# Low weight parts of layer 1 formed once in layer 0 and loaded, and the depthwise convolution on VectorE split by even and odd positions

## The chip, the cores and the metric

The kernel runs on one core of one Trainium2 chip. The metric is the device time of one execution in microseconds (us). "Before" is the kernel without the change, "after" the kernel with it. A difference is given in per cent of the time before.

## The reference

The reference takes an activation of 2048 positions by 1024 channels through two layers, in float32. Each adds to its input a mixer's output that was normalised (RMSNorm before the mixer and after it). Layer 0 is attention over a window of 128 positions and a pooling mixer. The change touches the second layer, whose mixer is:

```
def odd_mixer(h, w_in, dw_w, dw_b, ln_g, ln_b, w_out):
    proj = h @ w_in
    a, b, gate = jnp.split(proj, [CONV_WIDTH, 2 * CONV_WIDTH], axis=-1)
    glu = a * jax.nn.sigmoid(b)
    conv = lax.conv_general_dilated(
        glu, dw_w.astype(glu.dtype), window_strides=(1,), padding=[(CONV_K - 1, 0)],
        dimension_numbers=('NWC', 'WIO', 'NWC'), feature_group_count=CONV_WIDTH)
    cf = conv.astype(jnp.float32) + dw_b.astype(jnp.float32)
    mu = jnp.mean(cf, axis=-1, keepdims=True)
    var = jnp.mean(jnp.square(cf - mu), axis=-1, keepdims=True)
    cn = (cf - mu) * lax.rsqrt(var + EPS) * ln_g.astype(jnp.float32) + ln_b.astype(jnp.float32)
    y = jax.nn.silu(cn).astype(h.dtype) * jax.nn.silu(gate)
    return y @ w_out
```

`w_in` is 1024 x 3072, `w_out` 1024 x 1024, and the convolution has 31 taps for each of the 1024 channels. The norm over channels needs the convolution of all channels before one position can be finished.

## The kernel before

**Halves and blocks.** Positions are worked in two halves of 1024 (`NH`), each of two blocks of 512 (`NB`). Channels lie on the 128 partitions, in eight tiles (`KT`). Layer 0 runs through both halves (`inproj0`, `outproj(0, half)`), then layer 1: `inproj1(0)`, `gates1(0)`, `inproj1(1)`, `gates1(1)`, and after these `outproj(1, 0)` and `outproj(1, 1)`. TensorE's order of matmuls is this order.

**A projection in three matmuls.** Every float32 operand of a projection is split in a high part in a reduced format and a low part, the rest. `w_load` fetches one weight tile (`wr`, 128 x 8 x 128, 512 KB) after the other, in the order of a list `wseq`, through three buffers. `w_split` copies it on ScalarE to `wh` (line 373) and subtracts on VectorE to get `wl` (line 374), two buffers each. `project` (line 385) then does for each of the eight channel tiles three matmuls: `wh` by the high part of the activation, `wh` by its low part, `wl` by its high part. A tile of layer 1's input projection or gates (`wc`) serves both blocks of a half, 48 matmuls of 512 columns; a tile of the output projection (`wo1`) serves one block, 24 matmuls. So the 24 `wc` tiles are loaded and split twice, and the eight `wo1` tiles four times: 80 tiles in layer 1. The last block of the kernel (`last_block`) goes by two parts of 256 columns and keeps its eight tiles.

**The convolution.** For each channel tile `inproj1` projects `b` and `a`, and `glu` multiplies them into a tile `gl`. Five of the eight channel tiles are convolved on VectorE (`conv_dve`, line 1027): one multiply-add over 1024 positions for each tap, into two sums in turn, and an add that writes the result in another order of positions. It is stored in DRAM (`cd`). The other three go through TensorE with Toeplitz matrices (`conv_pe`), result `ct`. `gates1` makes SiLU of the gate and stores it (`sg`).

**The norm.** `norms(half)` loads the eight results again (`s<-cd`, `s<-ct`), adds them up (column sums on TensorE, tile `a`), subtracts the mean, sums squares, and spreads the root by TensorE (`pt` are column sums, `pv` what is spread). `apply` scales, takes SiLU, multiplies by the gate (`s<-sg`), and splits the mixed tile into `hi` and `lo`. These mixed tiles are what `outproj(1, half)` multiplies; `ready` there holds each matmul group until its tile is there. `norms(1)` starts only when eight of the sixteen mixed tiles (eight channel tiles, two blocks) of half 0 are done, as `dones[0]` says (line 1159).

**Who sets the order.** The instructions' order on each engine is fixed when the program is built. The code is written as tasks that yield; a planner (class `Flow`, line 54) runs the tasks against estimated costs and due times, and emits each engine's list of instructions by priority and readiness. So a change in one task's work moves other tasks' instructions. All loads and stores go through SP's queue, in the order of its list, and an instruction there that waits for a buffer holds all behind it. As every instruction is recorded by one wrapper, all carry line L189 in the profile (L190 in the changed kernel), and tiles are told apart by names: `mm` is the PSUM bank of a projection, `s` any tile of the common pool `s4` (37 slots of 1056 floats), `t` a small tile of 512.

## Time and profile before

| what | value |
|---|---|
| time, median of 3 runs | 1501.53 us (1500.33 to 1501.77) |
| profiled execution, its own time | 1503.71 us |
| its span in the trace | 1500.8 us |
| mean granted clock of TensorE | 0.991 |
| TensorE busy | 1469.3 us (98%) |
| VectorE busy | 1250.2 us (83%) |
| ScalarE busy | 565.2 us (38%) |
| DMA, share of 16 engines | 39.3% |

The span runs from the first to the last instruction that the profiler recorded; 2.9 us of the profiled execution lie outside it. A share of busy time is a mean over stages: layer 0 ends at about 675 us, layer 1's projections and gates at about 1260, the output projection of half 0 at about 1377, and the last block starts at about 1440. The granted clock is TensorE's, in parts of its full 2.4 GHz; 0.50 is its lower level of 1.2 GHz.

### The profile page before, as it was taken

Reading aid. Unit: us, or ns where it says so; the run is one execution under the profiler, and the core shown is the slowest. Engines: PE = TensorE matmul, PEld = TensorE weight load, DVE = VectorE, ACT = ScalarE, POOL = GpSimd, SP = SyncE. Lnnn points to the kernel's source line nnn. Section 1 sums busy time; section 2 is a strip of 40 time slices with the busy share of each in tenths; the row PEclk is TensorE's granted clock in tenths of the full one; section 3 lists DMA queues with packets and bytes.
Section 4 is the critical chain, followed back from the end, with each engine's and each line's share of the span. In section 5 each row is a group of like instructions: output and inputs, shape, how many; then the busy total and the mean of one; then the engine's idle time right before and its main releaser. Section 6 shows DMA issues by size and latency. Waiting matters only on the chain.

```text
span 1500.8 us, 19112 instructions
## 1 busy us (share of the span) xinstructions
PE 1469.3 (98%) x7226; PEld 1193.0 (79%) x7226; DVE 1250.2 (83%) x1927; ACT 565.2 (38%) x1069; POOL 49.1 (3%) x65
## 2 busy tenths in 40 slices
PE   8999999999999999999999999999999999998997
PEld 6877778788877778788888888888888888776796
DVE  7888775777887766577899999999999999989885
ACT  6454432454444423454211123211212134666551
POOL 0000000000000000000100000000000000000000
PEclk9999999999999999999999999999999999999898
DMA  6112312455411101355421224422544744836574
GB/s 221 57 54 80 97 44 59 140 175 176 145 33 33 46 29 56 99 178 187 166 63 55 82 85 136 172 71 67 182 148 137 236 144 137 256 127 229 165 251 154
DMA packets 107468, 186.46 MB, mean 124 GB/s; under 512 B 32240, under 2 KB 56432, under 8 KB 107376
## 3 DMA queue, kind: packets, MB, share of 16 engines
q1 hardware_dynamic: 107376, 185.25, 39.3%
q8 instruction: 56, 0.92, 0.3%
q14 instruction: 36, 0.29, 0.1%
HBM read 146.42 MB, written 38.80 MB: 123 GB/s over the span
## 4 chain that ended last, share of the span: by engine, by line
PE 92%; DVE 3%; DMA 2%; ACT 1%; issue 1%; SPq 0%; POOL 0%; POOLq 0%; DVEq 0%; ACTq 0%
PE mm L189 81%; PE a L189 5%; PE pv L189 3%; PE pt L189 2%; DVE s L189 2%; DMA s<-in_toep 1%; DVE t L189 1%; DVE wl L189 0%; DMA s<-in_xn 0%; DMA gt<-s 0%; ACT s L189 0%; DMA s<-sg 0%; SPq L189 0%; ACT wh L189 0%; ACT t L189 0%
## 5 line engine op out<-in xcount | busy, mean ns | idle before, releaser
L189 PE MATMUL mm<-s,wh 128*128 128x512 f32 (+1 forms) x3616 | 1139.6, 396 | 13.3 <-ACT s L189 7.4
L189 PEld LDWEIGHTS mm<-s,wh 128*128 128x128 f32 x3616 | 669.5, 189 | 164.6 <-DVE s L189 10.7
L189 PE MATMUL mm<-s,wl 128*128 128x512 f32 (+1 forms) x1808 | 709.9, 393 | 0.0
L189 PEld LDWEIGHTS mm<-s,wl 128*128 128x128 f32 x1808 | 341.4, 189 | 76.2
L189 DVE SCALAR_TENSOR_TENSOR s<-s,packed,s 128x1024 f32<-128x1024 f32 x290 | 354.6, 1279 | 0.0
L189 ACT ACTIVATE wh<-wr 128x1024 fp32r<-128x1024 f32 (+1 forms) x138 | 145.4, 1054 | 368.8 <-PE mm L189 315.9
L189 DVE TENSOR_TENSOR wl<-wr,wh 128x1024 fp32r<-128x1024 f32 (+1 forms) x138 | 167.7, 1215 | 74.9 <-ACT wh L189 72.8
L189 ACT ACTIVATE t<-mm 128x512 f32<-128x512 f32 (+1 forms) x122 | 68.5, 562 | 98.6 <-PE mm L189 90.3
L189 DVE TENSOR_TENSOR t<-t,t 128x512 f32<-128x512 f32 (+1 forms) x131 | 86.2, 663 | 17.3 <-ACT t L189 15.4
L189 ACT ACTIVATE s<-mm 128x512 f32<-128x512 f32 (+1 forms) x116 | 67.9, 585 | 78.2 <-PE mm L189 70.8
L189 PE MATMUL a<-s,s 128*128 128x128 f32 (+2 forms) x592 | 90.5, 290 | 1.1 <-DMA s<-in_toep 0.9
L189 PEld LDWEIGHTS a<-s,s 128*128 128x128 f32 x592 | 81.1, 190 | 11.1 <-DMA s<-in_toep 2.8
L189 DVE TENSOR_TENSOR s<-s,s 128x512 f32<-128x512 f32 (+3 forms) x100 | 85.0, 874 | 3.3 <-DMA s<-ct 1.0
L189 ACT ACTIVATE s<-t 128x512 fp32r<-128x512 f32 (+1 forms) x52 | 48.8, 938 | 64.4 <-DVE t L189 64.1
L189 DVE TENSOR_TENSOR s<-t,s 128x512 fp32r<-128x512 f32 (+1 forms) x56 | 52.4, 935 | 22.1 <-ACT s L189 20.9
L189 ACT ACTIVATE t<-s 128x512 f32<-128x512 f32 x80 | 48.8, 628 | 50.7 <-DVE s L189 42.4
L189 DVE TENSOR_TENSOR t<-pt,packed 128x512 f32<-128x512 f32 x64 | 44.1, 690 | 28.4 <-PE pt L189 27.9
L189 ACT ACTIVATE s<-s,st 128x128 f32<-128x128 f32 x128 | 49.6, 389 | 25.0 <-DVE st L189 24.9
L189 POOL TENSOR_TENSOR rs<-ms,mhalf 128x4 f32<-128x4 f32 (+1 forms) x21 | 24.9, 1186 | 791.8 <-DVE ms L189 787.7
L189 DVE SCALAR_TENSOR_TENSOR s<-t,mm 128x512 f32<-128x512 f32 x48 | 40.1, 836 | 8.1 <-PE mm L189 6.2
L189 ACT ACTIVATE s<-xh 128x512 fp32r<-128x512 f32 x48 | 29.9, 630 | 39.9 <-DVE xh L189 39.5
L189 PEld LDWEIGHTS pv<-t,s 128*64 128x64 f32 x480 | 25.1, 136 | 23.2 <-issue 7.2
(100 smaller groups left out, 928.3 us busy)
## 6 DMA issues: line engine op xcount, KB each, us to landing
wr<-in_wo SPq DMA_DIRECT2D x64, 512.0 KB, 3.7
wr<-in_wc SPq DMA_DIRECT2D x48, 512.0 KB, 3.7
wr<-in_wa SPq DMA_DIRECT2D x27, 512.0 KB, 3.7
s<-in_toep SPq DMA_DIRECT2D x24, 384.0 KB, 4.3
xr<-in_xp SPq DMA_DIRECT2D x32, 256.0 KB, 4.1
x<-s SPq DMA_DIRECT2D x32, 256.0 KB, 3.2
xh<-x SPq DMA_DIRECT2D x32, 256.0 KB, 3.6
sg<-s SPq DMA_DIRECT2D x16, 512.0 KB, 4.8
```

What stands on the lines that cost most here:

```text
L189: fn(*args, **kw)
```

## The change

**Low parts.** A new task `w_lows`, of low priority and due from 60 us on, forms the low part of each of the 32 different weight tiles of layer 1 during layer 0: a load of 512 KB, a copy on ScalarE, a subtraction on VectorE, a store of 512 KB into DRAM (`wcl_*`, `wo1l_*`). In layer 1 `w_split` no longer subtracts: it loads the low part into the `wl` buffer by SP's queue, 80 times, and copies `wh` as before.

**Convolution by parity.** `gl` holds its even and its odd positions apart. With x0, x1 the two and w0, w1 the even and odd taps, `conv_dve` forms x0 + x1 and three filters of 512 positions with 16, 15 and 16 taps: ya = w0 * x0, yb = w1 * x1, yc = (w0 + w1) * (x0 + x1). One parity of the result is ya + yb (shifted), the other yc - ya - yb. That makes one add of 527 elements, 47 multiply or multiply-add instructions of 512 or 513, and three adds of 512, of which two write in the changed order, where 31 instructions of 1024 and one add of 1024 stood. `glu` of these channel tiles becomes two instructions of half size.

**The norm's start and priorities.** `norms(1)` starts at `gated`, when all projections and gates are emitted, and no longer asks for eight mixed tiles of half 0; its loads run at most two ahead of the sums, its blocks have a priority one lower, and taking a slot waits until four are free or `gated`.

The diff, without the sizes of packed constants and the layout of the carried positions:

```diff
--- before.py
+++ after.py
...
@@ -320,6 +321,24 @@
     for h in range(NH):
         wseq += [("wo1", f) for b in range(NB) for f in range(KT)]
     wraw, wready, last = [], [], set()
+    lows = [x for n, x in enumerate(wseq) if x[0] in ("wc", "wo1") and x not in wseq[:n]]
+    kept = {(name, i): dr.tile([P, KT, P], F32, tag=f"{name}l_{i}", name=f"{name}l_{i}") for name, i in lows}
+    formed = set()
+
+    def w_lows():
+        yield 60.0
+        for name, i in lows:
+            yield from until(lambda: avail["s4"] > 5)
+            raw = (yield from get("s4")).rearrange("p (k f) -> p k f", k=KT)
+            wl = (yield from get("s4", TH, F32R)).rearrange("p (k f) -> p k f", k=KT)
+            yield Q.dma_start(out=raw, in_=a[name][i])
+            yield A.activation(wl, raw, AF.Copy)
+            at = V.tensor_tensor(out=wl, in0=raw, in1=wl.bitcast(F32), op=ALU.subtract)
+            put(raw)
+            yield at
+            Q.dma_start(out=kept[name, i], in_=wl.bitcast(F32))
+            put(wl)
+            formed.add((name, i))
 
     def w_load(go):
         for n, (name, i) in enumerate(wseq):
@@ -370,8 +389,12 @@
             for j, ks in enumerate(WPARTS if n == len(wseq) else WHOLE):
                 yield from until(lambda: len(at) > j)
                 yield at[j]
+                if (name, i) in kept:
+                    yield from until(lambda: (name, i) in formed)
+                    Q.dma_start(out=wl.bitcast(F32), in_=kept[name, i])
                 yield A.activation(wh[:, ks], raw[:, ks], AF.Copy)
-                V.tensor_tensor(out=wl[:, ks], in0=raw[:, ks], in1=wh[:, ks].bitcast(F32), op=ALU.subtract)
+                if (name, i) not in kept:
+                    V.tensor_tensor(out=wl[:, ks], in0=raw[:, ks], in1=wh[:, ks].bitcast(F32), op=ALU.subtract)
                 if j == 0:
                     wready.append((name, i, wh, wl))
             put(raw)
@@ -580,6 +603,7 @@
     rb0 = {}
     flow.spawn(w_load(go), 0)
     flow.spawn(w_split(), 0)
+    flow.spawn(w_lows(), 6)
     for b in range(NB):
         flow.spawn(prep_first(b, hs, have, go), 1 + b)
     flow.wait(lambda: len(go) == NB)
...
@@ -612,6 +638,10 @@
         G.memset(low, -1.0e37)
         V.tensor_scalar(nsink, sinks, -1.0, None, op0=ALU.mult)
         V.tensor_scalar(dwb, dwb, 2.0, None, op0=ALU.mult)
+        V.tensor_scalar(dwb2, dwb, 2.0, None, op0=ALU.mult)
+        pairs_of = dwn[:, :, 1:].rearrange("p i (m r) -> p i m r", r=2)
+        V.tensor_tensor(out=dws[:, :, 1:], in0=pairs_of[:, :, :, 0], in1=pairs_of[:, :, :, 1], op=ALU.add)
+        V.tensor_copy(dws[:, :, :1], dwn[:, :, :1])
         V.tensor_scalar(dwbp, dwbp, 2.0, None, op0=ALU.mult)
         yield at
         V.tensor_copy(upper, up[:, :P])
@@ -1024,22 +1054,38 @@
         for w in ws:
             put(*w)
 
+    def parities(gl):
+        return gl.rearrange("f (r j) -> f r j", r=2)
+
     def conv_dve(half, i, slot, gl, over):
-        acc = []
-        for _ in range(2):
-            acc.append((yield from get("s4")))
-        V.tensor_scalar(acc[0], gl[:, 0:TH], dwn[:, slot, 0:1], dwb[:, i:i + 1], op0=ALU.mult, op1=ALU.add)
-        yield flow.t["P"]
-        V.tensor_scalar(acc[1], gl[:, 1:1 + TH], dwn[:, slot, 1:2], None, op0=ALU.mult)
-        for k in range(2, CK):
-            yield flow.t["P"]
-            r = acc[k % 2]
-            V.scalar_tensor_tensor(r, gl[:, k:k + TH], dwn[:, slot, k:k + 1], r, op0=ALU.mult, op1=ALU.add)
+        n = TH // 2
+        even, odd = parities(gl)[:, 0, :], parities(gl)[:, 1, :]
+        ta = yield from get("s4", 2 * n + HJ)
+        tb = yield from get("s4", 2 * n + 1)
+        both, ya = ta[:, :n + HJ], ta[:, n + HJ:]
+        yb, yc = tb[:, :n + 1], tb[:, n + 1:]
+        V.tensor_tensor(out=both, in0=even, in1=odd, op=ALU.add)
+        for m in range(HJ + 1):
+            for r, x, w, bias in ((ya, even, dwn[:, slot, HIST - 2 * m:CK - 2 * m], dwb), (yb, odd, dwn[:, slot, HIST - 1 - 2 * m:HIST - 2 * m] if m < HJ else None, None), (yc, both, dws[:, slot, HJ - m:HJ + 1 - m], dwb2)):
+                if w is None:
+                    continue
+                yield flow.t["P"]
+                xs = x[:, HJ - 1 - m:HJ + n - m] if x is odd else x[:, HJ - m:HJ + n - m]
+                if m:
+                    V.scalar_tensor_tensor(r, xs, w, r, op0=ALU.mult, op1=ALU.add)
+                elif bias is None:
+                    V.tensor_scalar(r, xs, w, None, op0=ALU.mult)
+                else:
+                    V.tensor_scalar(r, xs, w, bias[:, i:i + 1], op0=ALU.mult, op1=ALU.add)
         put(gl)
         cf = yield from get("s4")
+        cv = cf.rearrange("f (q r s) -> f r s q", r=2, s=SG)
         yield flow.t["P"]
-        at = V.tensor_tensor(out=permuted(cf), in0=natural(acc[0]), in1=natural(acc[1]), op=ALU.add)
-        put(*acc)
+        V.tensor_tensor(out=cv[:, 0], in0=ya.rearrange("f (s q) -> f s q", s=SG), in1=yb[:, :n].rearrange("f (s q) -> f s q", s=SG), op=ALU.add)
+        V.tensor_tensor(out=ya, in0=ya, in1=yb[:, 1:], op=ALU.add)
+        yield flow.t["P"]
+        at = V.tensor_tensor(out=cv[:, 1], in0=yc.rearrange("f (s q) -> f s q", s=SG), in1=ya.rearrange("f (s q) -> f s q", s=SG), op=ALU.subtract)
+        put(ta, tb)
         yield at
         Q.dma_start(out=cd_t[i, half], in_=cf)
         put(cf)
...
@@ -1089,13 +1135,16 @@
         put(bank)
         ths[b] = th
 
-    def glu(bank, at, ths, b, gv, n):
+    def glu(bank, at, ths, b, gl, gv, n):
         yield at
         yield from until(lambda: b in ths)
         th = ths[b]
-        at = V.scalar_tensor_tensor(
-            gv[:, b * PB:(b + 1) * PB, :], th.rearrange("f (p s) -> f p s", p=PB), 1.0,
-            bank.rearrange("f (p s) -> f p s", p=PB), op0=ALU.add, op1=ALU.mult)
+        if gv is None:
+            at = V.scalar_tensor_tensor(gl[:, cols(b)], th, 1.0, bank, op0=ALU.add, op1=ALU.mult)
+        else:
+            for r in range(2):
+                tr, br = (t.rearrange("f (q r s) -> f q r s", r=2, s=SG)[:, :, r] for t in (th, bank))
+                at = V.scalar_tensor_tensor(gv[:, b * PB // 2:(b + 1) * PB // 2, r], tr, 1.0, br, op0=ALU.add, op1=ALU.mult)
         put(th, bank)
         n[0] = at
         n[1] += 1
...
@@ -1138,12 +1187,13 @@
         yield A.activation(c, c, AF.Silu, bias=lnb[:, k:k + 1], scale=lng[:, k:k + 1])
         key = (k // 2, b)
         if key not in sgs:
-            yield from until(lambda: (half, *key) in stored)
+            yield from until(lambda: (half, *key) in stored and (avail["s4"] > 3 or gated))
             g = yield from get("s4")
             sgs[key] = (g, Q.dma_start(out=g, in_=sg_t[(half, *key)]))
         g, at = sgs[key]
         yield at
         yield V.tensor_tensor(out=c, in0=c, in1=halves(g)[k % 2], op=ALU.mult)
+        yield from until(lambda: avail["s4"] > 3 or gated)
         t = yield from get("s4", TH, F32R)
         mix[b][k] = t
         hi, lo = halves(t)
@@ -1156,12 +1206,12 @@
                 put(tile)
 
     def norms(half, over, mix, done):
-        yield from until(lambda: len(over[half]) >= 5 and (half == 0 or len(dones[half - 1]) >= KT))
-        cfs, rbs, sgs, left, loaded = {}, {}, {}, {}, []
+        yield from until(lambda: len(over[half]) >= 5 and (half == 0 or gated))
+        cfs, rbs, sgs, left, loaded, added = {}, {}, {}, {}, [], [0]
 
         def load():
             for n in range(KT):
-                yield from until(lambda: len(over[half]) > n)
+                yield from until(lambda: len(over[half]) > n and added[0] >= n - 2)
                 k = over[half][n]
                 c = yield from get("s4")
                 if k in DVE_CONV:
@@ -1179,20 +1229,21 @@
             c, at = loaded[n]
             yield at
             V.tensor_tensor(out=total, in0=loaded[0][0] if n == 1 else total, in1=c, op=ALU.add)
+            added[0] = n
         cfs["sum"] = total
         yield flow.t["V"]
 
         def block(b):
             yield from norm_block(b, cfs, rbs)
-            yield from spread_tasks([apply(half, k, b, cfs, rbs, sgs, mix, done, left) for k in range(KT)], 3, 1 + b)
+            yield from spread_tasks([apply(half, k, b, cfs, rbs, sgs, mix, done, left) for k in range(KT)], 3, 1 + b + half)
             put(rbs[b])
 
         for b in range(NB):
-            flow.spawn(block(b), 1 + b)
+            flow.spawn(block(b), 1 + b + half)
         yield from until(lambda: len(rbs) == NB)
         put(total)
 
-    stored = set()
+    stored, gated = set(), []
 
     def gate_out(half, j, b, sg, ready):
         yield from until(lambda: ready[0] == 2)
@@ -1211,13 +1262,13 @@
             dve = i in DVE_CONV
             gl = grab("s4", TH + HIST if dve else TH)
             if dve:
-                G.tensor_copy(gl[:, :HIST], gc[:, DVE_CONV.index(i), :])
-                gv = gl[:, HIST:].rearrange("f (s p) -> f p s", p=PH)
+                G.tensor_copy(parities(gl)[:, :, :HJ], gc[:, DVE_CONV.index(i), :].rearrange("f (r j) -> f r j", r=2))
+                gv = parities(gl)[:, :, HJ:].rearrange("f r (s q) -> f q r s", q=PH // 2)
             else:
-                gv = gl.rearrange("f (p s) -> f p s", p=PH)
+                gv = None
             w = take("wc", i)
             for b in range(NB):
-                flow.spawn(glu(*project(w, pairs(hs), b), ths, b, gv, n), 0)
+                flow.spawn(glu(*project(w, pairs(hs), b), ths, b, gl, gv, n), 0)
             put(*w)
             flow.spawn(after_glu(half, i, gl, n, over), 1)
 
@@ -1256,6 +1307,7 @@
             for h in range(NH):
                 flow.spawn(norms(h, over, mixes[h], dones[h]), 1)
         gates1(half, now)
+    gated.append(1)
     for half in range(NH):
         outproj(1, half, mixes[half], dones[half])
     flow.wait(lambda: not flow.tasks)
...
```

**What moves.** On TensorE, in `outproj(1, 0)` block 0, the column sums for the mean of half 1 (`a<-s,ones`) stood in the eighth and last weight tile of the block, 186 weight matmuls after its start. Before:

```order
L189 MATMUL mm_10424<-s_1575_10073,wh_10391 128x512 x2
L189 MATMUL mm_10424<-s_1575_10073,wl_10392 128x512
L189 MATMUL a_1642_10456<-s_1584_10142,ones 128x512
L189 MATMUL a_1644_10461<-s_1584_10142,ones 128x512
L189 MATMUL mm_10424<-s_1582_10132,wh_10391 128x512 x2
L189 MATMUL mm_10424<-s_1582_10132,wl_10392 128x512
```

In the changed order they stand in its sixth tile (`wl_10760` is the low part of `wo1` tile 5), 129 weight matmuls after the start:

```order
L190 MATMUL mm_10798<-s_1614_10287,wl_10760 128x512
L190 MATMUL mm_10798<-s_1615_10302,wh_10759 128x512 x2
L190 MATMUL mm_10798<-s_1615_10302,wl_10760 128x512
L190 MATMUL a_1699_10826<-s_1647_10560,ones 128x512
L190 MATMUL a_1700_10828<-s_1647_10560,ones 128x512
L190 MATMUL mm_10798<-s_1623_10358,wh_10759 128x512 x2
```

The sums moved ahead by 57 weight matmuls. The eight `lo` subtractions of half 1's block 0 on VectorE, which complete the mixed tiles, stood between 360 and 405 weight matmuls after the same start, six of them behind the first matmul of `outproj(1, 1)` (at 384); after the change all are between 276 and 372.

On SP at the start of `outproj(1, 0)`, before: the loads of half 1's norm stand behind each other with one weight load on either side (`in_wo` is the weight matrix, `cd` and `ct` are results of the convolution, `sg` gates).

```order
L189 DMA wr_10114<-in_wo 128x1024
L189 DMA sg_3_1_103<-s_1559_9963 128x1024
L189 DMA s_1585_10143<-cd_1_79 128x1024
L189 DMA s_1586_10145<-ct_75 128x16x64
L189 DMA s_1587_10147<-cd_1_81 128x1024
L189 DMA s_1588_10149<-ct_76 128x16x64
L189 DMA s_1589_10151<-cd_1_83 128x1024
L189 DMA s_1590_10153<-cd_1_85 128x1024
L189 DMA s_1591_10155<-ct_77 128x16x64
L189 DMA s_1594_10167<-sg_1_1_91 128x1024
L189 DMA wr_10185<-in_wo 128x1024
```

After: the first low part that is loaded here is that of `wo1` tile 1 (`wo1l_133`), and five loads and a store lie between it and that of tile 2 (`wo1l_134`).

```order
L190 DMA wl_10556<-wo1l_133 128x1024
L190 DMA wr_10566<-in_wo 128x1024
L190 DMA s_1651_10573<-cd_1_79 128x1024
L190 DMA s_1652_10575<-ct_75 128x16x64
L190 DMA s_1653_10577<-cd_1_81 128x1024
L190 DMA s_1655_10582<-sg_0_1_89 128x1024
L190 DMA s_1656_10584<-sg_1_1_91 128x1024
L190 DMA sg_3_1_103<-s_1632_10442 128x1024
L190 DMA wl_10612<-wo1l_134 128x1024
L190 DMA wr_10622<-in_wo 128x1024
L190 DMA s_1663_10634<-cd_1_83 128x1024
L190 DMA s_1664_10643<-ct_76 128x16x64
```

Each weight tile now has two loads, and the norm's loads stand between the pairs. On SP at the start of the last block (`wo1l_132` is tile 0, the `128x4x256` loads fetch the block's input x), after:

```order
L190 DMA wl_11785<-wo1l_132 128x1024
L190 DMA wr_11795<-in_wo 128x1024
L190 DMA s_1886_11818<-x_1_1_107 128x4x256
L190 DMA s_1887_11819<-x_1_1_107 128x4x256
L190 DMA wl_11827<-wo1l_133 128x1024
L190 DMA wr_11842<-in_wo 128x1024
L190 DMA s_1894_11845<-wo1l_134 128x1024
L190 DMA wr_11865<-in_wo 128x1024
```

Before, the same place had the two loads of x and `wr` loads alone; the low part of tile 1 now stands behind the loads of x.

## Rows read from the trace of the kernel before

**Rows 1.** The page, part 1: busy us (share of the span) and instructions.

```profile
PE 1469.3 (98%) x7226; PEld 1193.0 (79%) x7226; DVE 1250.2 (83%) x1927; ACT 565.2 (38%) x1069; POOL 49.1 (3%) x65
```

**Rows 2.** Windows: length; busy PE, PEld, DVE, ACT, POOL; clock; DMA share; GB/s.

```profile
0.00:675.00 675.00, 664.25 (x3402) 526.68 (x3403) 501.88 (x1078) 299.53 (x639) 19.34 (x32) 1.00 0.31 95
675.00:952.00 277.00, 277.00 (x1220) 226.88 (x1219) 255.68 (x267) 69.15 (x100) 14.48 (x13) 1.00 0.37 117
952.00:1260.00 308.00, 306.97 (x1473) 253.54 (x1472) 291.24 (x278) 72.24 (x131) 5.77 (x12) 1.00 0.45 139
...
1377.40:1404.00 26.60, 19.16 (x58) 13.65 (x57) 21.88 (x39) 12.04 (x18) 2.83 (x2) 0.68 0.53 188
1404.00:1440.00 36.00, 36.00 (x159) 29.32 (x158) 32.27 (x47) 22.59 (x35) 0.00 (x0) 1.00 0.72 231
```

**Rows 3.** Groups of PE, 1377.4 to 1404: busy, mean ns, idle ahead.

```profile
L189 PE MATMUL mm<-s,wh 128*128 128x512 f32 x25 | 12.8, 570 | 3.7 <-DVE s L189 3.2 <-ACT s L189 0.5
L189 PE MATMUL mm<-s,wl 128*128 128x512 f32 x13 | 6.5, 502 | 0.0
L189 PE MATMUL pt<-ones,t 128*128 128x1 f32 x16 | 3.4, 332 | 3.7 <-DVE t L189 3.7
L189 PE MATMUL pv<-s,onesr 128*128 128x512 f32 x4 | 1.7, 511 | 0.0
```

**Rows 4.** Chain, 1370 to 1410: start us, us, what.

```profile
1380.66 5.31 DMA s<-sg
```

**Rows 5.** Windows, columns as in rows 2.

```profile
1000.00:1050.00 50.00, 50.00 (x217) 40.56 (x217) 48.86 (x44) 7.01 (x9) 0.00 (x0) 1.00 0.24 68
1380.00:1390.00 10.00, 3.80 (x12) 2.71 (x13) 9.04 (x17) 4.07 (x7) 1.44 (x1) 0.77 0.77 271
1390.00:1400.00 10.00, 8.79 (x24) 6.08 (x22) 7.87 (x17) 3.89 (x6) 1.39 (x1) 0.50 0.14 52
```

**Rows 6.** Waits of PE, 675 to 1375: us in total, times, longest.

```profile
PE mm L189 <- DVE s L189: 1.4, 2, 0.8
```

**Rows 7.** Groups of DVE by form, whole span.

```profile
L189 DVE SCALAR_TENSOR_TENSOR s<-s,packed,s 128x1024 f32<-128x1024 f32 x290 | 354.6, 1279 | 0.0
L189 DVE TENSOR_TENSOR wl<-wr,wh 128x1024 fp32r<-128x1024 f32 x136 | 166.3, 1223 | 71.3 <-ACT wh L189 69.2 <-DMA x<-s 0.9
...
L189 DVE SCALAR_TENSOR_TENSOR s<-s,packed,t 128x512 f32<-128x512 f32 x56 | 40.1, 746 | 4.0 <-ACT t L189 4.0
L189 DVE TENSOR_TENSOR s<-s,s 128x1024 f32<-128x1024 f32 x24 | 37.2, 1556 | 1.4 <-DMA s<-ct 1.0
L189 DVE TENSOR_TENSOR s<-s,xr 128x512 f32<-128x512 f32 x56 | 37.0, 686 | 2.3 <-DMA xr<-in_xp 1.8
...
L189 DVE TENSOR_SCALAR s<-s,packed 128x1024 f32<-128x1024 f32 x20 | 15.0, 777 | 0.0
```

**Rows 8.** Groups of ACT by form, whole span.

```profile
L189 ACT ACTIVATE wh<-wr 128x1024 fp32r<-128x1024 f32 x136 | 144.2, 1060 | 366.0 <-PE mm L189 315.9 <-issue 45.1 <-DMA xr<-in_xp 2.5
```

**Rows 9.** The page, part 6: DMA issues, KB each, median us to landing.

```profile
wr<-in_wo SPq DMA_DIRECT2D x64, 512.0 KB, 3.7
```

**Rows 10.** Tile sg, 1277 to 1279: issues, then the time to landing.

```profile
L189 SPq DMA_DIRECT2D s<-sg x2: 384/524/664, 1277.5 to 1278.0; - x2
L189 SPq DMA_DIRECT2D sg<-s x1: 319/319/319, 1277.1 to 1277.1; - x1
...
DMA to landing us min/median/max: 4.5/5.3/6.1
```

**Rows 11.** Tile x, 1437 to 1439: the same.

```profile
L189 SPq DMA_DIRECT2D s<-x x2: 425/462/498, 1437.6 to 1438.0; - x2
...
DMA to landing us min/median/max: 5.1/6.3/8.2
```

**Rows 12.** Windows, columns as in rows 2.

```profile
1290.00:1300.00 10.00, 10.00 (x45) 8.17 (x44) 9.74 (x11) 4.58 (x8) 0.00 (x0) 1.00 1.16 313
10.00:20.00 10.00, 9.43 (x28) 7.16 (x29) 9.15 (x14) 10.00 (x17) 0.00 (x0) 1.00 1.04 413
```

11 lines of the change are left out of this document (7 added, 4 removed).

## The prediction

> **What bounds the kernel now.** I read the page first: TensorE is busy 1469.3 of 1500.8 us [rows 1], so at most some 31 us of the span are TensorE not computing, and a gain has to come from those, from stretches at a low clock, or nowhere. The table of stretches shows where they are [rows 2]. In layer 1's two input projections and gates (675 to 1260 us) TensorE is busy 277.00 of 277.00 and 306.97 of 308.00 us. VectorE is nearly full there too (255.68 and 291.24 us), but nobody waits for it: making VectorE lighter buys nothing in these 585 us themselves. The loss stands in one place, 1377.4 to 1404.0: 19.16 of 26.60 us busy at a granted clock of 0.68. That is the start of the output projection of half 1 (`outproj(1,1)`).
>
> What TensorE does in those 26.60 us is 25 + 13 weight matmuls, 16 narrow column sums and 4 spread matmuls [rows 3]. The idle column there says who was late: VectorE's `s` (3.2 us) and `t` (3.7 us). The chain of waits through it shows the mixed tiles of half 1 still being made on VectorE, with a load of a gate tile, `s<-sg`, of 5.31 us between [rows 4]. In windows of 10 us TensorE falls to 3.80 us of work at clock 0.77, then works at 0.50, the lower of its two levels (1.2 GHz) [rows 5], and is back at full by 1404 [rows 2]. Everywhere between 675 and 1375 TensorE waits 1.4 us for VectorE in all [rows 6].
>
> **The change, part by part.** *The stall.* At full clock a 512-wide matmul costs 50.00/217 = 0.230 us [rows 5]. The 42 wide matmuls of [rows 3] are 9.7 us; the 16 narrow ones I take at half of that each, 1.8 us. So this stretch needs 11.6 us and takes 26.6: **15.0 us** to win if the mixed tiles of half 1 are ready. They will be, I think, for two reasons. VectorE loses work in layer 1: 80 of the weight subtractions at 1.223 us are 97.8 us, of which 48 lie before 1260 and 16 in the output projection of half 0, where they stood among the norm's instructions; and each convolution goes from 29 x 1.279 + 2 x 0.78 + 2.0 = 40.7 us (the last add writes in another order; of the 24 adds of 1024 the 14 plain ones take about as long as a weight subtraction, which leaves 2.0 for the 10 others) to 44 instructions of 512 (0.746 each) + 3 scalings (0.5) + 3 or 4 adds (0.7 to 1.0) = about 37.7 us, ten times, 30 us [rows 7]. Then the norm of half 1 no longer waits for mixed tiles of half 0: in the changed order its column-mean matmul stands 57 weight matmuls (13 us) earlier, and all its eight block-0 `lo` subtractions stand ahead of the first matmul that needs them, where in the order before all but two stood after. The lower end is 10 us (only the waits and half of the clock's loss go), the upper 15.
>
> *Small waits* for VectorE between 675 and 1375 [rows 6]: 1.0 us won, 0 to 1.4.
>
> *The low parts become loads.* In layer 1 each of 80 weight tiles now needs a second transfer of 512 KB on SP's queue, and this one can't be fetched ahead as the raw tile can: there are two `wl` buffers, so it is issued when the tile before the current one is finished, and is wanted by the third matmul of the next tile. Alone such a transfer lands in 3.7 us [rows 9]. A projection tile of 48 matmuls lasts 11.06 us, so I cost the 48 `wc` loads at nothing; their cover is 7 us each. A tile of the output projection has 24 matmuls, 5.53 us: cover 1.8 us + two matmuls (0.46), and any queue of two transfers ahead eats it. Three transfers of 512 KB issued between 1277.1 and 1278.0 landed after 4.5 to 6.1 us [rows 10], which is 1281.6 and 1284.1: each one ahead adds 1.25 us. The `s<-ct` loads, in pieces of 64 elements, are dearer: in the clump that holds them the queue moved 313 GB/s [rows 12], 1.68 us per 512 KB, and if the plain ones there cost 1.25, a `ct` costs about 2.4 (an estimate).
>
> Now the start of `outproj(1,0)` in the changed order of SP, counted from the end of the tile before (T = 0): `wl` of tile 1 and `wr`, then `cd`, `ct`, `cd`, two gate loads, a gate store, and only then `wl` of tile 2. That is eight at 1.25 and one at 2.4 = 12.4 us of transfers, plus what a lone one takes beyond its own 1.25 (2.45 us): it lands at 14.9. TensorE wants it at 2 x 5.53 + 0.46 = 11.5: **a wait of 3.3 us**. Carried on in the same way, tile 3 (behind `wr`, `cd`, `ct`) waits 0.6, tile 4 nothing, tile 5 (behind `ct`, `sg`, `cd`) 1.3. Sum 5.2; with every transfer at 1.68 it would be 11, with the loads served in time 0. Later in half 0's second block a gate load, `xr` loads and outputs share the queue: 1.0 (0 to 4).
>
> The Trainium skill, page "DMA: Bandwidth & Descriptors", section "Anatomy of one DMA", fits one transfer as 2.0 us plus its bytes at 436 GB/s; 512 KB would take 3.2 us by that (an estimate from the page), 0.5 less than the row, and nothing of what stands ahead in the queue is in it. By that alone no tile would wait, which is rival A below.
>
> *The last block* works in columns of 256, so that a tile lasts 2.8 us. Its tile 1 `wl` stands behind two loads of x, which in the trace landed 6.3 and 8.2 us after issue [rows 11] (the 5.1 there is an `xr` load ahead of them). If these are issued about 2 us ahead of the block, as there, `wl` lands about 5.2 us after its start and is wanted at 3.1: 2.1 us; if they are issued with it, 4.5. I take 3.0.
>
> *The clock.* A wait of 3.7 us of TensorE (its idle in front of `pt`, [rows 3]) was followed by the low level until near 1404: 8.79 us of work at 0.50 in 1390 to 1400 alone [rows 5], a loss of 4.4 us. I expect the same once, after the 3.3 us wait of tile 2, at 4.0; but the matmuls then run slowly while the queue catches up, so the 1.9 us of tiles 3 and 5 disappear: net **2.1** (0 to 5).
>
> *Layer 0* gets 32 subtractions (39.1 us of VectorE at 1.223), 32 copies on ScalarE (33.9 at 1.060) [rows 7, 8], and 64 transfers. VectorE is busy 501.88 of 675 us there, ScalarE 299.53, DMA at a share of 0.31 [rows 2], and the new instructions are spread over its output projections and gates, where TensorE leads. I charge 1.0 (-1 to 4): the cover is slack of 173 us, and if it fails in one tile, it costs a subtraction.
>
> Sum: -15.0 - 1.0 + 5.2 + 1.0 + 3.0 + 2.1 + 1.0 = **-3.7 us**. The profiled execution took 1503.71, span 1500.8 and 2.9 around it; 1500.8 - 3.7 = 1497.1, with 2.9 it is 1500.0, 2.2 above the median of the runs shown as before (1503.71 against 1501.53). Against that median: **1497.8**. A difference under 0.2%, 3 us, can't be told from none here.
>
> **Rivals.** *A, the low parts land in time* (SP runs further ahead than I think, or the `cd` loads start late): then only -15.0 - 1.0 + 1.0 is left, 1486.5. For it: alone a load has 1.8 us of cover. Against: five loads and a store between two `wl` in SP's order.
>
> *B, the queue is the new bound* (the slower side): 1404 to 1440 already moves 231 GB/s [rows 2], and 512 KB more per 5.53 us are 95 more, 326 in all. The Trainium skill, page "SBUF — State Buffer", section on the DMA setup-cost knee, gives 358 GB/s as the limit of HBM for a core; by that a 512 KB transfer takes 1.46 us (an estimate from the page) and my waits of 5.2 grow to some 8. Against it the trace has 413 GB/s in one window, though 313 in the one with `ct` [rows 12]. If transfers cost 1.5 to 1.7 us here, the waits for `wl` come to about 10 + 3 + 4.5 and the clock falls twice, 8: 1501.53 - 15 + 25 = 1511; with the clock falling twice at my own waits 1503. It decides from 15 us of waits and clock in all.
>
> *C, the stall stays*: the eight tiles of half 1 are also held by their `sg` loads, which stand in the same queue (5.31 us on the chain [rows 4]) now with twice the weights. Then nothing is won and the waits are paid: 1501.5 + 9 = 1510.
>
> *D, nothing to tell*: half the stall goes and the waits eat it, 1501.
>
> **How the numbers follow.** My own case (1494 to 1501) 0.45, of it 0.30 faster by over 0.2%, 0.13 within, 0.02 slower; A 0.16; B 0.21 (0.03 of it within); C 0.08; D 0.10 (0.08 within, 0.02 slower). Faster 0.46, same 0.24, slower 0.30. The range leaves out the lower half of A and the upper half of B and C: 1486 to 1508; my own case alone, 1494 to 1501.
>
> **What would show it.** No idle in front of `pt` and clock 1.00 at the start of `outproj(1,1)`; VectorE's share in 675 to 1260 down from 93% to about 78%, with TensorE unchanged there; TensorE waits on `wl` loads of some 3 us in the third tile of `outproj(1,0)` and in the last block, and a granted clock under 1 behind the first. Layer 0 as long as before, 675 us within 3. I am wrong if `wl` waits are absent or in every tile, or if the wait for VectorE at half 1's first tile survives.

## The result, and the profile after

The changed kernel took 1512.49 us (median of 4 runs, 1508.57 to 1514.18) against 1501.65 (1500.33 to 1502.59). The ratio of the means is 1.0069, with a 95% interval of 1.0046 to 1.0092. It is slower by 0.7%; forecast were 1497.8, 1486 to 1508. The profiled execution took 1513.91, its span is 1512.1.

The page of the changed kernel: busy time, the group of weight matmuls by `wl` with what they waited for, and the loads of `wl` in the output projection.

```profile
PE 1471.2 (97%) x7226; PEld 1194.4 (79%) x7226; DVE 1154.5 (76%) x2092; ACT 594.3 (39%) x1101; POOL 39.3 (3%) x65
...
L190 PE MATMUL mm<-s,wl 128*128 128x512 f32 (+1 forms) x1808 | 712.7, 394 | 17.2 <-DMA wl<-wo1l 17.2
...
wl<-wo1l SPq DMA_DIRECT2D x26, 512.0 KB, 4.6
```

VectorE lost 96 us of work against [rows 1], TensorE has the same 7226 instructions, and the span is 11.3 us longer. TensorE's 17.2 us of waits on `wl<-wo1l` are new. VectorE's groups after (by form):

```profile
L190 DVE SCALAR_TENSOR_TENSOR s<-s,dws,s 128x512 f32<-128x512 f32 x150 | 112.1, 748 | 0.0
...
L190 DVE SCALAR_TENSOR_TENSOR s<-s,packed,s 128x513 f32<-128x513 f32 x140 | 104.7, 749 | 0.0
...
L190 DVE TENSOR_TENSOR wl<-wr,wh 128x1024 fp32r<-128x1024 f32 x62 | 75.9, 1224 | 35.3 <-ACT wh L190 33.7 <-DMA wr<-in_wo 1.0
...
L190 DVE TENSOR_TENSOR s<-s 128x527 f32<-128x527 f32 x10 | 7.1, 706 | 0.1
```

The multiply-adds of half length take 747 to 749 ns, 440 of them (a third group of 150, not shown, has 747), as costed from [rows 7]; 62 full subtractions into `wl` are left of 136 (the last block's tiles stand under `s`). VectorE's prices held.

Where the time went is read by place in the program: both traces have the same weight matmuls, so the start of the n-th is the same place in each. Lengths in us of one profiled execution each, worked out from these starts (the last stretch ends with the last weight matmul):

| stretch | before | after - before | forecast |
|---|---|---|---|
| layer 0 | 709.2 | -5.5 | +1.0 |
| projections and gates of layer 1 | 573.2 | +6.1 | 0 |
| output projection, half 0 | 95.0 | +17.9 | +7.3 |
| half 1, first 48 weight matmuls | 29.3 | -16.9 | -15.0 |
| half 1, rest of block 0 | 33.2 | +4.8 | 0 |
| last block | 47.9 | +4.9 | +3.0 |

Windows after, cut at these places, and one of 8 us behind the longest wait (columns as in [rows 2]):

```profile
0.00:703.70 703.70, 695.73 (x3547) 553.75 (x3548) 552.76 (x1140) 340.62 (x692) 19.30 (x32) 1.00 0.43 143
703.70:1282.90 579.20, 575.23 (x2648) 471.13 (x2647) 460.62 (x713) 143.51 (x230) 13.28 (x26) 1.00 0.55 179
1282.90:1395.80 112.90, 100.43 (x419) 79.89 (x418) 85.38 (x140) 66.82 (x103) 3.33 (x3) 0.94 0.81 275
1300.00:1308.00 8.00, 7.32 (x24) 5.92 (x25) 5.39 (x7) 3.38 (x5) 0.00 (x0) 0.72 1.10 356
1395.80:1408.30 12.50, 12.50 (x60) 10.30 (x59) 9.57 (x18) 9.08 (x15) 1.01 (x1) 1.00 0.74 250
1408.30:1446.30 38.00, 35.35 (x146) 28.07 (x145) 15.88 (x25) 14.05 (x22) 0.00 (x0) 0.96 0.81 280
```

The stall of [rows 2] (19.16 of 26.60 us at clock 0.68) is gone: 12.50 of 12.50 at 1.00. About 1.5 us of the 16.9 (an estimate from their mean times) are only work that moved: eight column sums and two spread matmuls now stand in half 0's stretch and are part of its 17.9. But the output projection of half 0 now has 100.43 of 112.90. Its waits, of them those from 1360 us on, then those of the projections ahead of it and of all that follows (in total, times, longest):

```profile
PE mm L190 <- DMA wl<-wo1l: 11.6, 4, 6.1
```

```profile
PE mm L190 <- DMA wl<-wo1l: 4.9, 2, 2.7
```

```profile
PE a L190 <- DMA s<-in_toep: 3.9, 6, 1.1
```

```profile
PE mm L190 <- DMA wl<-wo1l: 5.5, 3, 2.9
```

SP's timeline after, at the start of that stretch (start, us, issues; `x2` are two), and the tile `wl` that is issued at 1292.53:

```profile
1283.09 0.32 SPq L190 DMA_DIRECT2D wl<-wo1l  x1
1284.00 0.33 SPq L190 DMA_DIRECT2D wr<-in_wo  x1
1284.39 0.42 SPq L190 DMA_DIRECT2D s<-cd  x1
1284.85 0.53 SPq L190 DMA_DIRECT2D s<-ct  x1
1285.43 5.58 SPq L190 DMA_DIRECT2D s<-cd  x1
1291.05 0.91 SPq L190 DMA_DIRECT2D s<-sg  x2
1292.05 0.38 SPq L190 DMA_DIRECT2D sg<-s  x1
1292.53 0.48 SPq L190 DMA_DIRECT2D wl<-wo1l  x1
1293.10 0.49 SPq L190 DMA_DIRECT2D wr<-in_wo  x1
1293.64 0.50 SPq L190 DMA_DIRECT2D s<-cd  x1
1294.19 0.70 SPq L190 DMA_DIRECT2D s<-ct  x1
1294.99 8.09 SPq L190 DMA_DIRECT2D wl<-wo1l  x1
```

```profile
  PE mm L190: 6.1, 1
...
DMA to landing us min/median/max: 8.1/8.1/8.1
```

This is the place that the prediction counted through. `wl` of tile 2 was to land 14.9 us after the stretch's start; it landed 8.1 us after 1292.53, 17.5 us after the first issue at 1283.09. Two things were worse than counted: eight transfers landed between 1287.4 (issue at 1283.09 and 4.3 us) and 1300.6, 1.66 us each where the sum has 1.39; and they started later, since `wr` is issued 0.9 us behind `wl`. The issue instructions of 5.58 and 8.09 us show that SP itself was held up (what goes with it stands in the last section). TensorE then ran at clock 0.72 (the window 1300 to 1308); tile 2 took 8.1 us more than before, 6.1 of wait and 2.0 for the clock, where 4.0 were forecast for it.

It was not the only fall of the clock. Four more follow, each behind a wait on a low part (2.2, 2.7, 2.1 and 2.9 us):

```profile
1368.00:1374.00 6.00, 5.97 (x19) 4.77 (x20) 6.00 (x11) 3.87 (x7) 0.00 (x0) 0.72 0.87 296
1388.00:1394.00 6.00, 4.92 (x15) 3.88 (x16) 6.00 (x11) 2.17 (x5) 0.00 (x0) 0.72 0.92 370
1432.00:1440.00 8.00, 6.02 (x19) 4.83 (x20) 0.69 (x1) 1.34 (x3) 0.00 (x0) 0.79 0.66 232
1452.00:1460.00 8.00, 7.59 (x49) 7.50 (x50) 2.21 (x7) 3.35 (x5) 1.01 (x1) 0.79 1.02 411
```

Each costs some 1.7 us of work ((1 - 0.72) x 6.00, (1 - 0.79) x 8.00). So the clock took 2.0 + 4 x 1.7 = 8.7 us, 5.3 of them in half 0. Half 0's 17.9 us are then 11.6 of waits, 5.3 for the clock and about 1.5 of moved work, less 0.5 of small waits that went.

### The profile page after: what moved, and what is told of

Its sections match the earlier page's. It is cut to its first block, busy times and chain, and to the rows that moved or that the text cites. A ratio compares the mean times of both kernels' runs of the same rounds, so it can differ in the third digit from the quotient of the medians.

```text
span 1512.1 us, 19557 instructions
## 1 busy us (share of the span) xinstructions
PE 1471.2 (97%) x7226; PEld 1194.4 (79%) x7226; DVE 1154.5 (76%) x2092; ACT 594.3 (39%) x1101; POOL 39.3 (3%) x65
## 5 line engine op out<-in xcount | busy, mean ns | idle before, releaser
L190 PE MATMUL mm<-s,wl 128*128 128x512 f32 (+1 forms) x1808 | 712.7, 394 | 17.2 <-DMA wl<-wo1l 17.2
L190 DVE SCALAR_TENSOR_TENSOR s<-s,packed,s 128x512 f32<-128x512 f32 (+1 forms) x290 | 207.0, 748 | 0.0
L190 DVE TENSOR_TENSOR s<-s,s 128x512 f32<-128x512 f32 (+4 forms) x152 | 132.3, 889 | 34.1 <-DMA s<-sg 12.8
L190 DVE SCALAR_TENSOR_TENSOR s<-s,dws,s 128x512 f32<-128x512 f32 x150 | 112.1, 748 | 0.0
L190 DVE SCALAR_TENSOR_TENSOR s<-t,mm 128x256 f32<-128x256 f32 (+1 forms) x68 | 42.3, 674 | 88.7 <-PE mm L190 84.2
L190 DVE TENSOR_TENSOR wl<-wr,wh 128x1024 fp32r<-128x1024 f32 (+1 forms) x64 | 77.3, 1207 | 39.1 <-ACT wh L190 37.4
L190 PEld LDWEIGHTS a<-s,s 128*128 128x128 f32 x592 | 81.0, 190 | 14.9 <-DMA s<-in_toep 7.5
L190 ACT ACTIVATE s<-s 128x1024 fp32r<-128x1024 f32 (+1 forms) x64 | 53.4, 844 | 44.6 <-DMA s<-in_wc 19.1
L190 DVE TENSOR_TENSOR s<-s,xr 128x512 f32<-128x512 f32 x56 | 37.3, 687 | 14.3 <-DMA xr<-in_xp 7.2
```

Source lines behind the costliest of these rows:

```text
L190: fn(*args, **kw)
```

## Experiments

Letters in the expectations: Q, low parts land late in SP's queue and TensorE's wait adds to the time; B, the DMA engines are full; V, P, W, which freed VectorE work took the stall away; N, the norm's earlier start did; S and L, the chain of half 1's norm sets the time whatever TensorE waits, and L: the transfers delay that chain. The table has each run's median, its ratio (of means) to the kernel before with interval, and by how many us the stretches of the table above were longer than before in the run's one profiled execution (0 layer 0, P projections, H0 output projection of half 0, S first 48 of half 1, R rest of block 0, E last block). That execution need not be a typical one: e5's was its fastest, 1504.75 us, e12's its slowest, 1505.77.

| run | us | ratio | 0 | P | H0 | S | R | E |
|---|---|---|---|---|---|---|---|---|
| (changed) | 1512.5 | 1.0069 [1.0046, 1.0092] | -5.5 | 6.1 | 17.9 | -16.9 | 4.8 | 4.9 |
| e1 | 1516.0 | 1.0102 [1.0083, 1.0120] | -5.2 | 5.4 | 6.4 | 3.9 | 0.0 | -0.2 |
| e2 | 1504.2 | 1.0029 [1.0018, 1.0041] | 3.9 | 0.5 | 11.2 | -16.0 | 0.9 | 0.6 |
| e3 | 1520.4 | 1.0132 [1.0116, 1.0147] | -1.8 | 1.8 | 12.0 | 5.0 | 0.3 | 0.1 |
| e4 | 1513.7 | 1.0076 [1.0049, 1.0102] | -5.4 | 11.4 | 12.4 | -14.5 | 3.1 | 3.0 |
| e5 | 1511.4 | 1.0062 [1.0040, 1.0084] | -3.8 | 2.0 | 13.8 | -16.5 | 4.0 | 2.5 |
| e6 | 1507.9 | 1.0050 [1.0034, 1.0066] | -5.7 | 3.2 | 3.1 | -3.6 | 0.0 | 5.7 |
| e7 | 1509.1 | 1.0058 [1.0040, 1.0077] | -5.3 | 4.6 | 16.1 | -16.8 | 2.3 | 3.5 |
| e8 | 1510.2 | 1.0071 [1.0044, 1.0098] | -5.8 | 4.0 | 8.8 | -10.7 | 4.8 | 6.4 |
| e9 | 1502.0 | 1.0009 [0.9999, 1.0018] | -5.0 | 5.6 | 6.5 | -9.4 | 2.5 | -0.1 |
| e10 | 1506.8 | 1.0042 [1.0027, 1.0057] | -0.6 | -1.6 | 9.9 | -12.0 | 0.0 | 7.3 |
| e11 | 1499.0 | 0.9988 [0.9979, 0.9997] | -4.7 | 5.5 | -0.4 | -12.2 | 2.3 | 5.7 |
| e12 | 1501.8 | 1.0007 [0.9998, 1.0016] | -3.9 | 4.6 | 18.6 | -16.8 | 0.2 | -0.2 |
| e13 | 1509.6 | 1.0062 [1.0047, 1.0077] | -5.2 | 5.4 | -0.7 | 2.2 | 0.3 | 4.0 |
| e14 | 1510.1 | 1.0066 [1.0051, 1.0081] | -2.0 | 1.4 | 4.1 | -17.3 | 1.9 | 19.7 |
| e15 | 1501.8 | 1.0010 [1.0001, 1.0020] | -5.7 | 2.4 | 12.4 | -16.5 | 2.0 | 4.6 |
| e16 | 1498.2 | 0.9986 [0.9977, 0.9995] | -5.2 | 3.5 | 11.9 | -15.8 | 2.2 | 0.0 |
| e17 | 1491.1 | 0.9932 [0.9918, 0.9945] | -5.3 | 2.9 | 6.1 | -16.9 | 1.7 | -0.2 |

**e1, e3, e5: which low parts.** The list `lows` is cut.

```diff
-    lows = [x for n, x in enumerate(wseq) if x[0] in ("wc", "wo1") and x not in wseq[:n]]
+    lows = [x ... if x[0] == "wc" and x not in wseq[:n]]      # e1; e5: "wo1"; e3: lows = []
```

> Only the 24 wc tiles keep a stored low part; the output projection's wo1 tiles are subtracted on VectorE as before. Theory Q (the loss is the low parts of wo1 arriving late in SP's queue): no wait on wl after 1283 us, the some 27 us that the output projections lost against the kernel before are back, 1485 to 1490. Rival V (the stall at half 1 went because VectorE was freed of the wo1 subtractions): the stall returns with 8 to 15 us, 1495 to 1502.

> No low part is stored or loaded; VectorE subtracts for all 80 tiles. The convolution by parity and the earlier norm stay. Theory N (the norm's earlier start removes the stall by itself): no stall at the start of the output projection of half 1, 1486 to 1492. Rival V (VectorE must be freed of the subtractions): a stall of 8 to 15 us stays there, 1495 to 1502.

> Only the eight wo1 tiles keep a stored low part; wc tiles are subtracted on VectorE as before. Theory W (the stall went because the output projection of half 0 was freed of its 16 subtractions, and the loss is the wait for these same loads): no stall at half 1's first tile, waits on wl of 15 to 22 us as in the changed kernel, 1503 to 1514. Rival P (the 48 subtractions taken out of the projections are needed too, since convolutions end earlier by them): the stall is back with over 8 us on top of the waits, over 1518.

Without the stored `wo1` parts there is no wait on `wl`, but the stall is there and larger (S +3.9, +5.0): V, not N, though both kernels are far slower than either expectation. Half 0 grew in them too (6.4 and 12.0 us), by waits for the norm's and the mixed tiles. With the `wo1` parts alone the stall is gone (S -16.5), the waits are nearly those of the changed kernel (14.3 us), and the time is W's. So in these three kernels the stall stays with the 16 subtractions in half 0 and is gone without them; e13 below shows that leaving them out is not enough by itself, and in e5 TensorE also came 13.8 us later to half 1. Whether the 48 `wc` loads, costed at nothing, cost anything is not shown. P grew by 4.4 us in the mean of the eleven kernels that have them on SP's queue with 37 slots, and by 2.5 in that of the four that have the new convolution without them (e3, e5, e12, e14). But about 1 us of this difference is work moved out of layer 0 (eight column sums), TensorE's waits for `s<-in_toep`, the Toeplitz loads of `conv_pe` (3.9 us in the changed kernel), are as long in e3 and e12 without these loads (3.2 and 3.6), and e5 and e12, one program up to there, grew by 2.0 and 4.6.

**e2, e4: cover and queue.** The edits of e2, then of e4:

```diff
-    "s4": 37, "t2": 5, "wr": 3, "wh": 2, "wl": 2, "xh": 2, "xr": 2, "ab": 1, "st": 3, "ms": 3, "rs": 2, "rh": 6,
+    "s4": 36, "t2": 5, "wr": 3, "wh": 2, "wl": 3, "xh": 2, "xr": 2, "ab": 1, "st": 3, "ms": 3, "rs": 2, "rh": 6,
...
+    QG = Engine(flow, "S", nc.gpsimd)
-                    Q.dma_start(out=wl.bitcast(F32), in_=kept[name, i])
+                    QG.dma_start(out=wl.bitcast(F32), in_=kept[name, i])
```

> All low parts as in the changed kernel, but three wl buffers (and 36 instead of 37 common slots), so that each load can be issued one tile earlier. Theory Q (late for want of cover): cover grows from 5.5 to 11 us, waits on wl fall from 17.2 to under 4 us, 1487 to 1494. Rival B (the DMA engines move all they can, so that an earlier issue doesn't help): waits stay above 10 us, over 1503.

> As the changed kernel, but the loads of low parts are issued by GpSimd, on its own queue, so that they don't stand behind the loads of cd, ct, sg and x on SP's. Theory Q (order in one queue): waits on wl under 6 us, 1488 to 1497. Rival B (the DMA engines are full): waits stay above 12 us, over 1505.

e2 does not test its theory: the task takes a `wh` buffer first, and of those there are still two, so no load is issued earlier. Its smaller waits (8.2 us) come with another order, and with 36 slots layer 0 is 9.4 us longer than in the changed kernel. In e4 the waits on `wl<-wo1l` fall to 9.7 us, but the time stays: others wait longer (`s<-in_toep` 5.9, `wl<-wcl` 2.3). Between both expectations; nearer to B.

**e6: low parts a tile earlier.** `w_load` fetches the low part next to the raw tile (`"wr": 2, "wl": 3`):

```diff
+            if (name, i) in kept and len(wseq) - n > KT - 2 and n != 2:
+                wl = yield from get("wl", dt=F32R)
+                yield from until(lambda: (name, i) in formed)
+                early[n] = wl
+                Q.dma_start(out=wl.bitcast(F32), in_=kept[name, i])
```

> As the changed kernel, but the low part is fetched by the task that fetches the raw tile, into three wl buffers (two raw buffers instead of three), so that it is issued one tile earlier and ahead of the norm's loads. Theory Q (late for want of cover): waits on wl under 5 us in all, no drop of the clock, 1484 to 1494. Rival B (the DMA engines are full): waits over 10 us, over 1502.

TensorE's loss in half 0 falls from 17.9 to 3.1 us (its waits on `wl` there from 11.6 to 2.6), and the stall is back: S -3.6 in place of -16.9. Q fails though these waits are nearly gone (one of 3.6 stays in the last block). Windows of e6 (columns as in [rows 2]), the shares of its chain from 1370 to 1397 with two links, and VectorE's two longest waits between 1280 and 1320:

```profile
1280.00:1320.00 40.00, 37.38 (x160) 29.46 (x159) 24.33 (x33) 22.67 (x35) 0.00 (x0) 1.00 0.98 322
1380.00:1395.00 15.00, 6.43 (x23) 3.60 (x22) 13.79 (x25) 7.96 (x13) 1.43 (x1) 0.79 0.62 245
```

```profile
by line: DVE s L190 46.5%; DMA s<-sg 29.3%; PE mm L190 12.4%; ACT s L190 4.7%; ACT wh L190 4.0%; issue 3.4%; SPq L190 1.2%; DVE ms L190 0.3%
...
1373.90 7.91 DMA s<-sg
...
1386.51 4.11 DVE s L190 x7
```

```profile
DVE s L190 <- DMA s<-ct: 7.3, 2, 6.2
DVE s L190 <- DMA s<-sg: 5.5, 4, 3.5
```

In the first 40 us VectorE has 24.33 us of work, with DMA at 0.98 of its engines; at the end it is at 13.79 of 15 and TensorE at 6.43. VectorE idles early for its loads and is late at the end, behind a gate load of 7.91 us: the mechanism of the prediction's rival C.

**e7, e8: the other two parts undone.** e7 has the convolution and `glu` of before, e8 the old condition in `norms`.

```diff
-        yield from until(lambda: len(over[half]) >= 5 and (half == 0 or gated))
+        yield from until(lambda: len(over[half]) >= 5 and (half == 0 or len(dones[half - 1]) >= KT))
```

> Low parts and the norm's start as in the changed kernel, the convolution and the gating product as before. Theory W (the convolution's 30 us lie on VectorE where nobody waits): within 4 us of the changed kernel, 1508 to 1517, stall gone. Rival P: convolutions of half 1 end later, the stall is back, over 1518.

> As the changed kernel, but the norm of half 1 starts when eight mixed tiles of half 0 are done, as before. Theory W: within 4 us of the changed kernel, 1508 to 1517, no stall. Rival N (the earlier start took the stall away): the stall is back with 8 to 15 us, 1518 to 1528.

Both within 4 us of the changed kernel: W. Neither 30 us less convolution nor the earlier norm is needed for the stall to go, though in e8, whose half 0 is 9 us shorter than the changed kernel's, 6 us of it stay (S -10.7).

**e9, e12, e16, e17: which tiles load.** A set `direct` names weight tiles of the output projection, counted over both halves, that are subtracted on VectorE again.

```diff
-                if (name, i) in kept:
+                if (name, i) in kept and len(wseq) - n not in direct:
...
-                if (name, i) not in kept:
+                if (name, i) not in kept or len(wseq) - n in direct:
...
+    direct = {first + t for t in (*range(7), *range(22, 32))}   # e9
```

> As the changed kernel, but the first seven weight tiles of the output projection of half 0 and the last ten of half 1 are subtracted on VectorE again, where low parts came late; the 15 others keep their loads. Theory Q (waits on wl add to the time one for one): about 11 us of waits and clock at the start, 5 before the last block and 4 in it go, 1490 to 1496. Rival S (the start of half 1's output projection is set by the chain of half 1's norm, whatever TensorE waits before it): the stall comes back as the waits go; only the 9 us at the end are won, 1498 to 1506.

> Stored low parts for the eight wo1 tiles alone, and loaded only in the 16 weight tiles of the output projection of half 0, where VectorE also makes half 1's norm; all wc tiles and half 1's wo1 tiles are subtracted on VectorE as before. Reading so far (wc loads cost some 4 us in the projections, half 1's loads some 9 us at the end, half 0's loads cost about what the stall gives back): no waits on wl after half 0, 1494 to 1503. Rival (VectorE falls behind again in half 1's block 0 when it subtracts there): the stall is back, over 1508.

e9 wins some 9 us on the changed kernel (by the ratios) but not on the one before: H0 falls by 11.4, S gives 7.5 of it back (S, the theory, in part). e12 (`wo1` parts only, loaded in half 0 only) is within its expectation. R and E are 0.2 and -0.2: half 1's own loads cost the changed kernel 9.7 us, half 0's buy the stall (18.6 against -16.8).

**e10: the kernel before, padded.**

```diff
+            if layer and half == 0 and b == 0:
+                pad = grab("mm")
+                hi = src(0, 0)[0]
+                for _ in range(48):
+                    T.matmul(pad, hi[:, :P], hi, start=True, stop=True)
+                    flow.pump()
+                put(pad)
```

> The kernel before with 48 more matmuls of 512 columns (11.1 us) at the start of the output projection of half 0, into a bank that nobody reads. Theory S: the stall at half 1 takes up most of them; no more than 4 us longer than before, under 1505. Rival Q: 8 to 11 us longer, 1508 to 1512.

Between the two: 6.0 us longer (0.42% by the means). The stall gives back 12.0 us, more than the 9.9 that half 0 grew by, as S has it, but the last block lost 7.3 in the new order of work.

**e11, e13: no low parts in half 0, and loads that nobody waits for.** In both the third matmul of half 0's 16 tiles takes `wh`; in e11 the load is left out too (the first two lines of the edit are e11's alone).

```diff
-                if (name, i) in kept:
+                if (name, i) in kept and len(wseq) - n not in bare:
-                    wready.append((name, i, wh, wl))
+                    wready.append((name, i, wh, wh if len(wseq) - n in bare else wl))
+                    spare[wh.name] = wl
```

> As the changed kernel, but in the 16 weight tiles of the output projection of half 0 the third matmul uses the high part once more, so that there is no low part to load or to subtract (the results of half 0 lose the low part's share). Theory Q: no waits on wl there and no stall, so 18 us less than the changed kernel, 1490 to 1495. Rival S: TensorE reaches half 1 some 18 us earlier and waits there for the norm's chain, of which at least 8 us remain, 1500 to 1508.

> As the changed kernel with all its loads, but in the 16 weight tiles of the output projection of half 0 the third matmul uses the high part again (the results lose the low part's share there), so that TensorE doesn't wait for the loads, which still take their place in the queue. Reading L (the transfers hold up half 1's norm, wherever TensorE waits): no waits on wl in half 0, and the stall at half 1 is back with 10 us or more, so that the time is within 5 us of the changed kernel, 1505 to 1513. Rival W (only the waits cost): as without the loads, 1496 to 1501.

The pair shows the price of the transfers apart from TensorE's wait. Windows of the kernel before, of e11, then of e13:

```profile
1282.40:1320.00 37.60, 36.79 (x160) 29.68 (x159) 36.07 (x43) 23.35 (x35) 0.00 (x0) 1.00 0.81 239
```

```profile
1283.00:1320.00 37.00, 36.93 (x157) 29.14 (x156) 25.48 (x35) 22.85 (x35) 0.00 (x0) 1.00 0.89 276
```

```profile
1282.00:1320.00 38.00, 38.00 (x167) 30.96 (x166) 24.75 (x34) 22.49 (x34) 0.00 (x0) 1.00 1.04 346
1375.00:1405.00 30.00, 18.03 (x53) 10.97 (x52) 27.90 (x48) 17.95 (x28) 1.32 (x1) 0.66 0.70 251
```

Without the loads, half 0 is as before and the stall 12.2 us shorter; some 4.6 us of it stay, and the time (1499.0) lies between the two expectations. With the loads present and not waited for, half 0 is as before too, and the stall is whole: TensorE 18.03 of 30.00 us at 0.66, VectorE 27.90. L holds: 16 transfers more in SP's queue (346 against 276 GB/s in the first stretch) go with 13.6 us more over H0 and S where TensorE waits on `wl` (the changed kernel against e11) and with 14.1 where it doesn't (e13 against e11), as a later norm; in the whole kernel's medians with 13.5 and 10.6. The planner's order of work differs between the kernels as well, so not all of it need be the transfers. And e13 has no subtractions in half 0 either. So the stall went in the changed kernel mainly because TensorE came to it 17.9 us later, as far as kernels of another order can show it.

**e14, e15: each half of the change alone.**

> The kernel before with the convolution by parity alone: no low parts stored, the norm as before. Reading: 30 us less on VectorE in the projections, where nobody waits; the convolutions of half 1 end earlier, and the stall at half 1 shrinks by 0 to 8 us, 1493 to 1502. Rival (the new order of work puts half 1's norm later, as with the convolution and the new start without low parts): over 1510.

> The kernel before with the low parts alone: the convolution and the norm as before. Reading: the same waits on wl as in the changed kernel (14 to 20 us), no stall, 1505 to 1514. Rival (the norm's later start brings the stall back on top): over 1516.

The convolution alone, 30 us less on VectorE, is 0.66% slower, as the rival had it; its stall is gone from half 1's first tile (S -17.3) and is back in the last block (E 19.7). Window and the longest link of the chain there:

```profile
1428.00:1452.00 24.00, 10.93 (x43) 7.73 (x42) 21.85 (x36) 12.46 (x19) 1.01 (x1) 0.62 0.68 240
```

```profile
1432.10 7.83 DMA xr<-x
```

The mixed tiles of half 1's block 1 are now late, behind an `xr` load of 7.83 us. The low parts alone are within 0.2% of before, faster than expected, with waits of 13.7 us and no stall. The parts don't add: the convolution alone is +0.66%, the low parts alone +0.10%, both with the norm's start +0.69%, and convolution and norm without the low parts +1.32% (e3).

**e16, e17: low parts alone, put where they pay.** From e15, `direct` holds the last block's eight tiles (e16), and also tiles 2 and 3 of half 0 (e17).

> The low parts alone (convolution and norm as before), but the last block's eight tiles are subtracted on VectorE as before. Reading: the wait on wl in the last block (2.9 us and what follows, 4.6 in all) goes and nothing else changes, 1496 to 1499. Rival: something else ends last in the block, 1501.

> As the run beside it, and weight tiles 2 and 3 of the output projection of half 0 are subtracted on VectorE too, where TensorE waited 8.8 us and more for the load behind the norm's loads. Theory Q (the waits add one for one): 10 to 13 us less, 1484 to 1489. Reading L (the section lasts as long as half 1's norm, whose loads fill the queue): the wait goes, a stall of some us returns at half 1, 1490 to 1499.

e16 wins 3.6 us on e15: the last block's 4.6 go, the rest is as it was. e17 beats both kernels: 1491.05 us, 0.68% under before (0.55 to 0.82%). Its waits on `wl`, and windows at the start of half 0 and of half 1:

```profile
PE mm L190 <- DMA wl<-wo1l: 4.9, 3, 3.3
```

```profile
1279.00:1320.00 41.00, 40.12 (x170) 31.40 (x169) 34.06 (x48) 25.95 (x41) 0.00 (x0) 1.00 0.88 278
1370.00:1400.00 30.00, 26.75 (x114) 21.47 (x113) 22.97 (x40) 16.90 (x26) 1.37 (x1) 0.94 0.85 306
```

Taking the wait of 8.9 us at tile 2 away won 7.1 us, less than Q's 10 to 13 since a wait of 3.3 us now stands at 1371, and no stall came back (S -16.9). The time lies in L's range, but no stall returned, which is Q's mechanism and against L here: VectorE has 34.06 of 41.00 us of work in the first stretch, where it had 24.33 of 40 in e6. With the old norm the loads of `cd` and `ct` go out in one clump ahead of the weight loads, which I take for the reason; it was not tried by itself.

## Why the prediction was wrong

- *The low parts become loads*: this step failed. For half 0 the terms were 5.2 + 1.0 + 2.1 - 1.0 for the small waits = 7.3 us, and 17.9 were measured. The first clump was near in its sum (6.7 us of waits for 5.2, though 6.1 of them at tile 2, where 3.3 were counted): the queue was counted at 1.39 us per transfer and gave 1.66. The second block of half 0, where gate loads, `xr` and outputs share the queue, was not: 4.9 us of waits in place of 1.0.
- *The clock, net 2.1*: mis-sized as well. The fall behind the longest wait cost 2.0, but there were five falls and 8.7 us, 5.3 of them in half 0.
- Rival B (1511) is what happened, in its time and in the sums of its terms: transfers of 1.5 to 1.7 us, 17.5 us of waits and 8 for the clock, against 1.66, 17.2 and 8.7. It was given 0.21. The limit of 358 GB/s that the Trainium skill gives for HBM per core (page "SBUF — State Buffer", section "The DMA setup-cost knee") was no bound here: the window 1300 to 1308 moved 356, but 1452 to 1460 moved 411, and [rows 12] has 413.
- The sum took the stall and the waits as separate, and in this kernel they aren't. Where the waits were taken away by themselves, the stall came back (e6, e13), since the same loads delay half 1's norm: rival C's mechanism, which the changed kernel hides behind TensorE's waits. With the old norm and convolution they were separate (e17).
- *The stall goes, 15.0*: right in size (16.9, less some 1.5 of moved work), but in part by luck. VectorE freed of 16 subtractions takes most of it away where no loads stand in their place (e11: S -12.2); with the loads it is whole in this kernel when TensorE doesn't wait ahead of it (e13). The convolution was not needed (e7; alone it moves the stall to the last block, e14), and the norm's earlier start little (e8: S -10.7 where half 0 is 9 us shorter).
- *"I cost the 48 `wc` loads at nothing"*: the projections grew by 6.1 us, 3.0 of it by longer waits for the Toeplitz loads and about 1 by work moved from layer 0. That the `wc` loads cause the rest or the waits is not shown; TensorE never waits there for `wl`.
- *Half 1's block 0*: not costed at all; 4.8 us, 2.6 of waits and 1.7 for the clock.
- *The last block, 3.0*: 4.9, its wait 2.9 us and 1.7 for the clock (in e16, which has no such wait, the block is as long as before).
- *Layer 0, +1.0*: -5.5, in every run with all 32 low parts between -4.7 and -5.8 save e2 with its 36 slots, and about -2 in e3 and e14, which form none. More work made it shorter: TensorE's waits there fell from 10.6 to 7.8 us, and about 1 us moved to the next stretch; the rest, and why the waits are shorter, is open. It nearly cancels the growth of the projections, so that the total came out near rival B's by some luck.
